# Deeper prefetch in the last loop of a hybrid encoder block: more buffers, gathered weights in halves, five splits on VectorE, a later fetch of the residual

## The chip, the cores and the metric

The kernel runs on one core of one Trainium2 chip. The metric is device time in microseconds of one execution; the median of several executions counts, and a profiled execution shows where the time goes.

## The reference

One encoder layer works on 512 tokens of width 1024, in float32. A mixer (a gated linear recurrence and a long convolution, merged by gates) adds to the tokens, then a PEER layer adds to them, then a last RMS norm follows. The change touches the PEER layer:

```python
def block(xb):
    T = xb.shape[0]
    qh = (xb @ w_q).astype(jnp.float32).reshape(T, PEER_HEADS, 2, PEER_QDIM // 2)
    s = jnp.einsum('thpc,hpnc->thpn', qh, sk)
    s1, i1 = lax.top_k(s[:, :, 0], PEER_TOPK)
    s2, i2 = lax.top_k(s[:, :, 1], PEER_TOPK)
    ...
    top_s, pos = lax.top_k(cand_s, PEER_TOPK)
    experts = jnp.take_along_axis(cand_i, pos, axis=-1)
    g = jax.nn.softmax(top_s, axis=-1).astype(xb.dtype)
    u = jnp.take(u_tab, experts, axis=0)
    v = jnp.take(v_tab, experts, axis=0)
    act = jax.nn.gelu(jnp.einsum('td,thkd->thk', xb, u)) * g
    return jnp.einsum('thk,thkd->td', act, v)
```

Each token picks 128 of 16384 experts (8 heads, 16 each). An expert is one row of table u and one row of table v, both of 1024 numbers.

## The kernel before

The 512 tokens are four blocks of 128. Three of them (`DTB`, 384 tokens) are computed densely: every expert is applied to every token, and a table of gates, zero where an expert was not chosen, weighs the result. The 16384 experts are 128 rows of 128 (`NK`); two rows are a pair, so there are 64 pairs. The fourth block (`GTB`) is computed by gathering: for each of the 128 choices of a token one row of u, later one row of v, comes by an indirect DMA.

For a row r, `act_row` loads a block of u (`uraw`), splits it into a high and a low part (`uh` on ScalarE, `ul` on VectorE, or on GpSimd once `looping` holds something), runs 24 matmuls into `ps_a` and writes the gelu of the result to `gact`. The ring for these results has eight tiles of a pair each. 22 pairs (`kept`, every third) are computed first and parked in DRAM; the others stay in the ring.

`gates_out` writes the gates of the dense blocks to DRAM as `Gd`. In the last loop `gated(p)` loads a block of gates `gt` (one for two pairs) and, for a kept pair, `gkept`; it multiplies both in place (L1013) and splits the product into `gh` and `gl`. `split_v(r)` loads row r of table v (`vraw`) and splits it into `vh` and `vl`, three rows ahead. `combine(r)` runs 18 matmuls into the six accumulators `acc`. Thus a plain row of the loop is 18 matmuls, and one with an act row 42; 70 of the act rows lie in the loop, over its first 120 rows. Six (`LEFT`) come just ahead of it: this stretch, in which the choice of the gathered block's experts (`select`) also runs on VectorE, is called the bridge below.

`gathered()` is the other side of the loop. It ends the choice for block `GTB`, then asks for the gathered rows, four ahead, one indirect DMA of GpSimd each, and works them up on VectorE: 128 dot products into `gdot` (L978), one gelu and one product with the gates (L980, L981), then 128 multiply-adds into `gacc` (L985, L987). `weave` runs both sides: each value that `rows()` yields lets through as many steps of `gathered()` as it counts, 2.08 (`WEIGHT`) for every row of the loop.

After the last act row `fetch_residual` asks for the final norm's weights and for the four blocks of tokens on ScalarE's queue. `summed` and `scaled` add, norm and store at the end.

The order on each engine is laid by a scheduler that estimates times: an instruction can stand ahead of one that the program names earlier, but each engine's queue, SP's list of DMA requests too, then runs strictly in its order, and an instruction that waits holds all behind it. A buffer of a pool is given again only when the last reader of its former tile is done. `issue_after` ties the gathers to the latest split on GpSimd.

Of the kernel before, what the change touches and what calls it, by code (L numbers as in the profile page):

```python
# [21 lines left out]
P = 128  # L22
# [795 lines left out]
GTB = 0  # L818
# [25 lines left out]
def peer(C, ctx, mh, ml):  # L844
# [4 lines left out]
    xg = cp.tile([P, D], F32, name="xg")  # L849
    gate = cp.tile([P, TB, P], F32, name="gate")  # L850
    eid = cp.tile([P, TB, P], F32, name="eid")
    v16 = cp.tile([P, TB, 16, TOPK], F32, name="v16")
    i16 = cp.tile([P, TB, 16, TOPK], U32, name="i16")
    pio = cp.tile([P, NPAIR, TOPK // 2], BF16, name="pio")
    with tc.tile_pool(name="pid", bufs=1) as ip:
        pid = ip.tile([P, NPAIR], F32, name="pid")
        nc.scalar.dma_start(pid, a["pair"].to_broadcast([P, NPAIR]))
        nc.vector.tensor_copy(pio, pid[:, :, None].to_broadcast([P, NPAIR, TOPK // 2]))
    iota = cp.tile([P, P, 4], BF16, name="iota")
    nc.gpsimd.iota(iota, pattern=[[1, P], [0, 4]], base=0, channel_multiplier=0, allow_small_or_imprecise_dtypes=True)  # L860
    gidx = cp.tile([P, P], I32, name="gidx")
    gdot = cp.tile([P, P], F32, name="gdot")
    gw = cp.tile([P, P], F32, name="gw")
    def chosen(pool, tb, part, ahead=2):
        return select(C, pool, tb, part, v16, i16, gate, eid, pio, ahead)

# [3 lines left out]
    puctx = ExitStack()  # L870
    sgctx = ExitStack()
    pu = puctx.enter_context(tc.tile_pool(name="pu", bufs=UB, side="right"))
    s0 = sgctx.enter_context(tc.tile_pool(name="sg", bufs=1, side="right")).tile([P, 16, P], F32, name="s0")
    acts, factors, looping = {}, {}, []
    anchor = [None]
    last_gelu = [None]
# [26 lines left out]
            nc.scalar.dma_start(C.kept[kept.index(r // 2)], acts.pop(r // 2))  # L903

    NP = NK // 2
    kept = [p for p in range(NP) if (p + 1) * KEPT // NP > p * KEPT // NP]
    order = [r for r in range(NK) if r // 2 in kept] + [r for r in range(NK) if r // 2 not in kept]

    def act_rows():
# [10 lines left out]
    with tc.tile_pool(name="gb", bufs=1) as gb, tc.tile_pool(name="slw", bufs=2) as sw, \  # L920
            tc.tile_pool(name="go", bufs=3) as go, tc.tile_pool(name="ps_g", bufs=5, space=PSUM) as ps_g:
        def best(pool):
            for hp in range(16):
                top16(C, pool, v16[:, GTB, hp], i16[:, GTB, hp], s0[:, hp])
                if hp % 2:
                    yield 0.4

        def weighed(tb, parts):
            for part in parts:
                for c in chosen(sw, tb, part):  # L930
                    yield CHOICE * c
# [27 lines left out]
    def gathered():  # L959

        for part in range(2):
            yield from chosen(sw, GTB, part, 1)
        nc.vector.tensor_copy(gidx, eid[:, GTB])
        swctx.close()
        gp = rowctx.enter_context(tc.tile_pool(name="gp", bufs=GBUFS))
        asked = chain(((a["u"], j) for j in range(P)), ((a["v"], j) for j in range(P)))
        there = []
        for q in islice(asked, GAHEAD):
            there.append(gather(gp, *q))
            yield 1.2  # L970

        def row():
            there.extend(gather(gp, *q) for q in islice(asked, 1))
            return there.pop(0)

        for j in range(P):
            t = row()
            nc.vector.scalar_tensor_tensor(t, t, 1.0, xg, op0=ALU.mult, op1=ALU.mult, accum_out=gdot[:, j : j + 1])  # L978
            yield 1.2
        nc.scalar.activation(gw, gdot, AF.Gelu_apprx_tanh)  # L980
        nc.vector.tensor_mul(gw, gw, gate[:, GTB])  # L981
        for j in range(P):
            t = row()
            if j == 0:
                nc.vector.tensor_scalar(gacc, t, gw[:, 0:1], None, op0=ALU.mult)  # L985
            else:
                nc.vector.scalar_tensor_tensor(gacc, t, gw[:, j : j + 1], gacc, op0=ALU.mult, op1=ALU.add)  # L987
            yield 1.2

    prep = {}  # L990
# [1 line left out]
    def split_v(r):  # L992
# [4 lines left out]
        split(nc, vh, vl, raw)  # L997
        prep[r] = vh, vl

    def gated(p):  # L1000

        r = 2 * p
        if r % GR == 0:
            gt = pg.tile([P, NG, GR * GQ], F32, name="gt")
            nc.sync.dma_start(gt, C.Gd[:, :, r * GQ : (r + GR) * GQ].rearrange("g p x -> p g x"))
            prep["gt"] = gt.rearrange("p g (r t) -> p r g t", t=GQ)
        if p in kept:
            g = pg.tile([P, 2, ND], F32, name="gkept", bufs=1)
            nc.sync.dma_start(g, C.kept[kept.index(p)])
        else:  # L1010
            g = acts.pop(p)
        g4 = g.rearrange("p r (g t) -> p r g t", t=GQ)
        nc.vector.tensor_mul(g4, g4, prep["gt"][:, r % GR : r % GR + 2])  # L1013
        gh = pg.tile([P, 2, ND], F32R, name="gh", bufs=3)
        gl = pg.tile([P, 2, ND], F32R, name="gl", bufs=3)
        split(nc, gh, gl, g)
        prep["g", p] = gh, gl
# [12 lines left out]
    def rows():  # L1030
        for r in range(AHEAD - 1):
            split_v(r)
        for _ in range(LEFT - 1):
            act_row()
            yield 2.4
        gated(0)
        act_row()
        split_v(AHEAD - 1)
        gated(1)
        yield 2.4  # L1040
        n = len(order)
        for r in range(NK):
            while order and (n - len(order)) * (NK - END) < (r + 1) * n:
                act_row()
                if not order:
                    log_table(C, last_gelu[0])
                    puctx.close()
                    fetch_residual()
            if r + AHEAD < NK:
                split_v(r + AHEAD)  # L1050
            if r % 2 == 0 and r // 2 + 2 < NP:
                gated(r // 2 + 2)
            if r < NK - LAST:
                combine(r)
            elif r == NK - 1:
                for k in range(len(DTB)):
                    for c in range(2):
                        for q in range(NK - LAST, NK):
                            combine(q, (k,), (c,))
            yield WEIGHT  # L1060

    fin = {}

    def fetch_residual():
        fin["pool"] = fp = rowctx.enter_context(tc.tile_pool(name="fin", bufs=1, side="right"))
        fin["g"] = gf = fp.tile([P, D], F32, name="gf")
        nc.scalar.dma_start(gf, a["g_fin"].to_broadcast([P, D]))
        for tb in range(TB):
            fin[tb] = fp.tile([P, D], F32, name=f"ht{tb}")
            nc.scalar.dma_start(fin[tb], C.hd[tb * P : tb * P + P])  # L1070

    looping.append(True)
    weave(rows(), gathered(), 1.0)


# [60 lines left out]
def queries(C, xh, xl, v16, i16, s0, chosen, fill):  # L1136
# [3 lines left out]
    with tc.tile_pool(name="slc", bufs=1) as cp, tc.tile_pool(name="slw0", bufs=2) as w2, tc.tile_pool(name="slw1", bufs=2) as sw:  # L1140
# [3 lines left out]
        def scores(hp, ps):  # L1144
            qT = w2.tile([P, L], F32, name="qT")
            nc.scalar.copy(qT, ps)
            pt = C.ps_s.tile([P, 512], F32, name="ps_s")
            for tb in range(TB):
                nc.tensor.matmul(pt[:, tb * P : tb * P + P], qT[:, tb * P : tb * P + P], sk[:, hp], start=True, stop=True)
            pt = pt.rearrange("p (t n) -> p t n", t=TB)  # L1150
            s = w2.tile([P, len(DTB), P], F32, name="s")
            nc.scalar.copy(s, pt[:, DTB[0] : DTB[-1] + 1])
            nc.scalar.copy(s0[:, hp], pt[:, GTB])
            for k, tb in enumerate(DTB):
                top16(C, w2, v16[:, tb, hp], i16[:, tb, hp], s[:, k])

        early = chain(*(chosen(sw, tb, 0) for tb in DTB[:EARLY]))
        for hp in range(16):
# [30 lines left out]
def select(C, w2, tb, part, v16, i16, gate, eid, pio, ahead=2):  # L1189
# [3 lines left out]
    hs = slice(part * 2 * H, part * 2 * H + 2 * H)  # L1193
    ks = slice(part * H * TOPK, part * H * TOPK + H * TOPK)
    i16f = w2.tile([P, 2 * H, TOPK], F32, name="i16f")
    nc.vector.tensor_copy(i16f, i16[:, tb, hs])
    ctop = w2.tile([P, H, TOPK], F32, name="ctop")
    cpos = w2.tile([P, H, TOPK], U32, name="cpos")
    cs = w2.tile([P, H, NPAIR], F32, name="cs")
    ci = w2.tile([P, H, NPAIR], F32, name="ci")  # L1200
    i1x = w2.tile([P, H, TOPK], F32, name="i1x")
    vv = v16[:, tb, hs].rearrange("p (h q) k -> p h q k", q=2)
    ii = i16f.rearrange("p (h q) k -> p h q k", q=2)
    nc.vector.tensor_scalar(i1x, ii[:, :, 0], 128.0, None, op0=ALU.mult)
    for dst, x1, x2, groups in ((cs, vv[:, :, 0], vv[:, :, 1], pair_groups(0, TOPK)[0]), (ci, i1x, ii[:, :, 1], FIRST + OTHERS)):
# [216 lines left out]
```

## Time and profile before

| | |
|---|---|
| median of 3 runs | 2085.55 us (2085.42 to 2086.84) |
| profiled execution | 2092.13 us |
| its span | 2090.4 us |
| first matmul into acc | 1250.5 us |
| last matmul into acc | 2083.0 us |
| granted TensorE clock, mean | 0.994 |

In the profile, PE is the matmuls of TensorE, PEld its weight loads, DVE is VectorE, ACT ScalarE, POOL GpSimd and SP the engine that only issues DMAs. Times count from the start of the span. A row of a timeline gives start and duration in us, the engine, the line, the operation, out<-in with shapes, and in brackets the idle time ahead of it with what ended it. A row of waits gives who waited for whom, the total in us, how often, and the longest. What a profiled execution takes above the median is not told apart by stage.

### The profile page before, as it was taken

Reading aid. Unit: us, or ns where it says so; the run is one execution under the profiler, and the core shown is the slowest. Engines: PE = TensorE matmul, PEld = TensorE weight load, DVE = VectorE, ACT = ScalarE, POOL = GpSimd, SP = SyncE. Lnnn points to the kernel's source line nnn. Section 1 sums busy time; section 2 is a strip of 40 time slices with the busy share of each in tenths; the row PEclk is TensorE's granted clock in tenths of the full one; section 3 lists DMA queues with packets and bytes.
Section 4 is the critical chain, followed back from the end, with each engine's and each line's share of the span. In section 5 each row is a group of like instructions: output and inputs, shape, how many; then the busy total and the mean of one; then the engine's idle time right before and its main releaser. Section 6 shows DMA issues by size and latency. Waiting matters only on the chain. (4 is left out here: it accounts for less than half of the span.)

```text
span 2090.4 us, 30873 instructions
## 1 busy us (share of the span) xinstructions
PE 2040.2 (98%) x11625; PEld 1791.7 (86%) x11625; DVE 1680.3 (80%) x3094; ACT 988.9 (47%) x1432; POOL 568.9 (27%) x336
## 2 busy tenths in 40 slices
PE   8999999999999999999999989999999999999996
PEld 6888888777777898889999988888888888888885
DVE  6788864898998647979999777897776787888795
ACT  5555434667766623436776643333333224333332
POOL 0000000000000000000000047767676666766860
PEclk9999999999999999999999999999999999999998
DMA  5212213122112444224556688999988998999984
GB/s 191 81 51 66 71 61 100 61 71 72 61 61 82 133 151 139 91 74 163 214 190 241 244 262 306 339 328 327 330 322 293 334 336 303 347 345 341 332 325 160
DMA packets 157844, 417.97 MB, mean 200 GB/s; under 512 B 12891, under 2 KB 66013, under 8 KB 156031
## 3 DMA queue, kind: packets, MB, share of 16 engines
q1 hardware_dynamic: 111900, 260.96, 36.4%
q0 software_dynamic: 36864, 134.23, 17.3%
q10 hardware_dynamic: 8930, 20.81, 2.8%
q8 instruction: 91, 1.49, 0.3%
q14 instruction: 59, 0.48, 0.1%
HBM read 377.94 MB, written 38.01 MB: 199 GB/s over the span
## 5 line engine op out<-in xcount | busy, mean ns | idle before, releaser
L93 POOL TENSOR_TENSOR ul<-uraw,uh 128x1024 fp32r<-128x1024 f32 x75 | 201.3, 2685 | 636.7 <-ACT uh L92 632.0
L101 PE MATMUL ps_a<-pxh,uh 128*128 128x384 f32 x1024 | 347.9, 340 | 8.4 <-ACT gact L901 8.4
L102 PE MATMUL ps_a<-pxl,uh 128*128 128x384 f32 x1024 | 345.1, 337 | 0.0
L1027 PE MATMUL acc<-vl,gh 128*128 128x512 f32 x768 | 302.1, 393 | 14.1 <-DVE vl L93 14.1
L1028 PE MATMUL acc<-vh,gl 128*128 128x512 f32 x768 | 302.0, 393 | 0.0
L1026 PE MATMUL acc<-vh,gh 128*128 128x512 f32 x768 | 300.4, 391 | 0.0
L92 ACT CAST vh<-vraw 128x1024 fp32r<-128x1024 f32 x128 | 134.6, 1051 | 350.3 <-DMA vraw<-in_v 241.3
L101 PE MATMUL ps_mm<-xh,whi 128*128 128x512 f32 (+1 forms) x656 | 256.9, 393 | 0.6 <-ACT gt L254 0.4
L102 PE MATMUL ps_mm<-xl,whi 128*128 128x512 f32 (+1 forms) x656 | 255.4, 391 | 0.0
L987 DVE SCALAR_TENSOR_TENSOR xg<-grow,gw,xg 128x1024 f32<-128x1024 f32 x127 | 188.9, 1487 | 57.3 <-DMA grow<-in_v,gidx 55.7
L978 DVE SCALAR_TENSOR_TENSOR grow<-grow,xg 128x1024 f32<-128x1024 f32 x128 | 177.8, 1406 | 53.6 <-DMA grow<-in_u,gidx 53.3
L101 PEld LDWEIGHTS ps_a<-pxh,uh 128*128 128x128 f32 x1024 | 193.2, 189 | 12.9 <-ACT gact L901 9.9
L860 POOL IOTA iota<- 128x512 bf16 x1 | 1.2, 1236 | 744.3 <-DVE gt L295 744.3
L955 POOL DMA_INDIRECT grow<-in_u,gidx x128 | 188.7, 1474 | 46.9 <-issue 22.3
L104 PE MATMUL ps_a<-pxh,ul 128*128 128x384 f32 x1024 | 198.2, 334 | 0.0
L102 PEld LDWEIGHTS ps_a<-pxl,uh 128*128 128x128 f32 x1024 | 193.2, 189 | 3.0
L92 ACT CAST whi<-wraw 128x1024 fp32r<-128x1024 f32 x112 | 117.5, 1050 | 156.6 <-PE ps_mm L102 133.6
L955 POOL DMA_INDIRECT grow<-in_v,gidx x128 | 177.4, 1386 | 38.6 <-issue 20.2
L93 DVE TENSOR_TENSOR vl<-vraw,vh 128x1024 fp32r<-128x1024 f32 x128 | 182.4, 1426 | 4.6 <-ACT vh L92 4.6
L1027 PEld LDWEIGHTS acc<-vl,gh 128*128 128x128 f32 x768 | 145.2, 189 | 43.9 <-DVE vl L93 14.9
L92 ACT CAST uh<-uraw 128x1024 fp32r<-128x1024 f32 x128 | 134.4, 1050 | 96.4 <-PE ps_a L102 66.8
L104 PEld LDWEIGHTS ps_a<-pxh,ul 128*128 128x128 f32 x1024 | 179.3, 188 | 0.1
(409 smaller groups left out, 4103.9 us busy)
## 6 DMA issues: line engine op xcount, KB each, us to landing
uraw<-in_uT SPq DMA_DIRECT2D x128, 512.0 KB, 5.6
vraw<-in_v SPq DMA_DIRECT2D x128, 512.0 KB, 6.4
wraw<-in_w_in SPq DMA_DIRECT2D x80, 512.0 KB, 3.6
Gd<-Gs SPq DMA_DIRECT2D x12, 2048.0 KB, 7.8
gt<-Gd SPq DMA_DIRECT2D x32, 768.0 KB, 8.9
kept<-gact ACTq DMA_DIRECT2D x22, 384.0 KB, 3.7
gkept<-kept SPq DMA_DIRECT2D x22, 384.0 KB, 5.1
wraw<-in_w_q SPq DMA_DIRECT2D x16, 512.0 KB, 4.6
```

Of the source, the lines that this page charges most:

```text
L92: nc.scalar.copy(hi, src)
L93: return (eng or nc.vector).tensor_sub(lo, src, hi).ins
L101: nc.tensor.matmul(out, ah, bh, start=(i == 0), stop=False)
L102: nc.tensor.matmul(out, *((al, bh) if late else (ah, bl)), start=False, stop=False)
L104: nc.tensor.matmul(out, *((ah, bl) if late else (al, bh)), start=False, stop=(stop and i == n - 1))
L860: nc.gpsimd.iota(iota, pattern=[[1, P], [0, 4]], base=0, channel_multiplier=0, allow_small_or_imprecise_dtypes=True)
L955: nc.gpsimd.indirect_dma_start(out=t, out_offset=None, in_=tab, in_offset=bass.IndirectOffsetOnAxis(ap=gidx[:, j : j + 1], axis=0))
L978: nc.vector.scalar_tensor_tensor(t, t, 1.0, xg, op0=ALU.mult, op1=ALU.mult, accum_out=gdot[:, j : j + 1])
L987: nc.vector.scalar_tensor_tensor(gacc, t, gw[:, j : j + 1], gacc, op0=ALU.mult, op1=ALU.add)
L1026: nc.tensor.matmul(acc[k][c], gh[:, ts_], vh[:, ds_], start=(r == 0), stop=False)
L1027: nc.tensor.matmul(acc[k][c], gh[:, ts_], vl[:, ds_], start=False, stop=False)
L1028: nc.tensor.matmul(acc[k][c], gl[:, ts_], vh[:, ds_], start=False, stop=(r == NK - 1))
```

## The change

Only the PEER layer changes.

- `gt` has three buffers in place of two and `gkept` two in place of one. Their loads move out of `gated` into `fetched(p)`, which is called four pairs ahead (`FETCH`); the first four calls stand ahead of `gated(0)`.
- The first and second best of the dense blocks (`v16`, `i16`) and `iota` move to a pool that is closed before the last loop.
- The list of kept pairs is mirrored: 0, 3, ... 61 in place of 2, 5, ... 63.
- `looping` is set after `gated(0)` in place of before the bridge, so the splits that the first five of the six bridge rows ask for run on VectorE.
- A row of the loop yields in proportion to its estimated matmul time, with the same total.
- `gdot` and `gw` are halves of 64 columns, each with its own gelu and its own product with the gates, the product 16 rows later.
- `fetch_residual` is called behind `split_v(127)`, and issues on SP.

```diff
 WEIGHT = 2.08
+COMB = 18 * 227
+ACTR = 24 * 173
...
+FETCH = 4
+LATER = 16
...
-    v16 = cp.tile([P, TB, 16, TOPK], F32, name="v16")
-    i16 = cp.tile([P, TB, 16, TOPK], U32, name="i16")
+    v16 = {GTB: cp.tile([P, 16, TOPK], F32, name="v16g")}
+    i16 = {GTB: cp.tile([P, 16, TOPK], U32, name="i16g")}
...
-    iota = cp.tile([P, P, 4], BF16, name="iota")
-    nc.gpsimd.iota(iota, pattern=[[1, P], [0, 4]], base=0, channel_multiplier=0, allow_small_or_imprecise_dtypes=True)
...
-    gdot = cp.tile([P, P], F32, name="gdot")
-    gw = cp.tile([P, P], F32, name="gw")
+    gdot = [cp.tile([P, P // 2], F32, name=f"gdot{h}") for h in range(2)]
+    gw = [cp.tile([P, P // 2], F32, name=f"gw{h}") for h in range(2)]
...
-    s0 = sgctx.enter_context(tc.tile_pool(name="sg", bufs=1, side="right")).tile([P, 16, P], F32, name="s0")
+    sg = sgctx.enter_context(tc.tile_pool(name="sg", bufs=1, side="right"))
+    for tb in DTB:
+        v16[tb] = sg.tile([P, 16, TOPK], F32, name=f"v16{tb}")
+        i16[tb] = sg.tile([P, 16, TOPK], U32, name=f"i16{tb}")
+    iota = sg.tile([P, P, 4], BF16, name="iota")
+    nc.gpsimd.iota(iota, pattern=[[1, P], [0, 4]], base=0, channel_multiplier=0, allow_small_or_imprecise_dtypes=True)
+    s0 = sg.tile([P, 16, P], F32, name="s0")
...
-    kept = [p for p in range(NP) if (p + 1) * KEPT // NP > p * KEPT // NP]
+    kept = [p for p in range(NP) if (NP - p) * KEPT // NP > (NP - 1 - p) * KEPT // NP]
...
+        half = P // 2
+
+        def weigh(h):
+            nc.vector.tensor_mul(gw[h], gw[h], gate[:, GTB, h * half : h * half + half])
+
         for j in range(P):
             t = row()
-            nc.vector.scalar_tensor_tensor(t, t, 1.0, xg, op0=ALU.mult, op1=ALU.mult, accum_out=gdot[:, j : j + 1])
+            h, i = divmod(j, half)
+            nc.vector.scalar_tensor_tensor(t, t, 1.0, xg, op0=ALU.mult, op1=ALU.mult, accum_out=gdot[h][:, i : i + 1])
+            if i == half - 1:
+                nc.scalar.activation(gw[h], gdot[h], AF.Gelu_apprx_tanh)
+            if j == half + LATER:
+                weigh(0)
             yield 1.2
-        nc.scalar.activation(gw, gdot, AF.Gelu_apprx_tanh)
-        nc.vector.tensor_mul(gw, gw, gate[:, GTB])
         for j in range(P):
...
+            if j == LATER:
+                weigh(1)
             yield 1.2
...
+    def fetched(p):
+
+        r = 2 * p
+        if p < NP and r % GR == 0:
+            gt = pg.tile([P, NG, GR * GQ], F32, name="gt", bufs=3)
+            nc.sync.dma_start(gt, C.Gd[:, :, r * GQ : (r + GR) * GQ].rearrange("g p x -> p g x"))
+            prep["gt", r // GR] = gt.rearrange("p g (r t) -> p r g t", t=GQ)
+        if p in kept:
+            g = prep["k", p] = pg.tile([P, 2, ND], F32, name="gkept")
+            nc.sync.dma_start(g, C.kept[kept.index(p)])
+
     def gated(p):
 
         r = 2 * p
-        if r % GR == 0:
-            gt = pg.tile([P, NG, GR * GQ], F32, name="gt")
-            nc.sync.dma_start(gt, C.Gd[:, :, r * GQ : (r + GR) * GQ].rearrange("g p x -> p g x"))
-            prep["gt"] = gt.rearrange("p g (r t) -> p r g t", t=GQ)
-        if p in kept:
-            g = pg.tile([P, 2, ND], F32, name="gkept", bufs=1)
-            nc.sync.dma_start(g, C.kept[kept.index(p)])
-        else:
-            g = acts.pop(p)
+        g = prep.pop(("k", p)) if p in kept else acts.pop(p)
+        gt = prep["gt", r // GR]
...
         for _ in range(LEFT - 1):
             act_row()
             yield 2.4
+        for p in range(FETCH):
+            fetched(p)
         gated(0)
+        looping.append(True)
         act_row()
         split_v(AHEAD - 1)
         gated(1)
         yield 2.4
         n = len(order)
+        share = (WEIGHT * NK) / (COMB * NK + ACTR * n)
         for r in range(NK):
+            time = COMB
             while order and (n - len(order)) * (NK - END) < (r + 1) * n:
                 act_row()
+                time += ACTR
                 if not order:
                     log_table(C, last_gelu[0])
                     puctx.close()
-                    fetch_residual()
             if r + AHEAD < NK:
                 split_v(r + AHEAD)
-            if r % 2 == 0 and r // 2 + 2 < NP:
-                gated(r // 2 + 2)
+            if r + AHEAD == NK - 1:
+                fetch_residual()
+            if r % 2 == 0:
+                fetched(r // 2 + FETCH)
+                if r // 2 + 2 < NP:
+                    gated(r // 2 + 2)
...
-            yield WEIGHT
+            yield share * time
...
-        nc.scalar.dma_start(gf, a["g_fin"].to_broadcast([P, D]))
+        nc.sync.dma_start(gf, a["g_fin"].to_broadcast([P, D]))
         for tb in range(TB):
             fin[tb] = fp.tile([P, D], F32, name=f"ht{tb}")
-            nc.scalar.dma_start(fin[tb], C.hd[tb * P : tb * P + P])
-
-    looping.append(True)
+            nc.sync.dma_start(fin[tb], C.hd[tb * P : tb * P + P])
+
     weave(rows(), gathered(), 1.0)
```

More of the change, by code (lines that the diff above doesn't have):

```diff
@@ L923, in best @@
             for hp in range(16):
-                top16(C, pool, v16[:, GTB, hp], i16[:, GTB, hp], s0[:, hp])
+                top16(C, pool, v16[GTB][:, hp], i16[GTB][:, hp], s0[:, hp])
                 if hp % 2:
@@ L974, in row @@
             return there.pop(0)
+        half = P // 2
+        def weigh(h):
+            nc.vector.tensor_mul(gw[h], gw[h], gate[:, GTB, h * half : h * half + half])
         for j in range(P):
             t = row()
-            nc.vector.scalar_tensor_tensor(t, t, 1.0, xg, op0=ALU.mult, op1=ALU.mult, accum_out=gdot[:, j : j + 1])
+            h, i = divmod(j, half)
[4 more added lines that the diff above has]
+                weigh(0)
             yield 1.2
-        nc.scalar.activation(gw, gdot, AF.Gelu_apprx_tanh)
-        nc.vector.tensor_mul(gw, gw, gate[:, GTB])
         for j in range(P):
             t = row()
+            h, i = divmod(j, half)
             if j == 0:
-                nc.vector.tensor_scalar(gacc, t, gw[:, 0:1], None, op0=ALU.mult)
+                nc.vector.tensor_scalar(gacc, t, gw[0][:, 0:1], None, op0=ALU.mult)
             else:
-                nc.vector.scalar_tensor_tensor(gacc, t, gw[:, j : j + 1], gacc, op0=ALU.mult, op1=ALU.add)
+                nc.vector.scalar_tensor_tensor(gacc, t, gw[h][:, i : i + 1], gacc, op0=ALU.mult, op1=ALU.add)
+            if j == LATER:
+                weigh(1)
             yield 1.2
@@ L998, in split_v @@
         prep[r] = vh, vl
+    def fetched(p):
[7 more added lines that the diff above has]
+            nc.sync.dma_start(g, C.kept[kept.index(p)])
     def gated(p):
         r = 2 * p
-        if r % GR == 0:
-            gt = pg.tile([P, NG, GR * GQ], F32, name="gt")
-            nc.sync.dma_start(gt, C.Gd[:, :, r * GQ : (r + GR) * GQ].rearrange("g p x -> p g x"))
-            prep["gt"] = gt.rearrange("p g (r t) -> p r g t", t=GQ)
-        if p in kept:
-            g = pg.tile([P, 2, ND], F32, name="gkept", bufs=1)
-            nc.sync.dma_start(g, C.kept[kept.index(p)])
-        else:
-            g = acts.pop(p)
+        g = prep.pop(("k", p)) if p in kept else acts.pop(p)
+        gt = prep["gt", r // GR]
         g4 = g.rearrange("p r (g t) -> p r g t", t=GQ)
-        nc.vector.tensor_mul(g4, g4, prep["gt"][:, r % GR : r % GR + 2])
+        nc.vector.tensor_mul(g4, g4, gt[:, r % GR : r % GR + 2])
         gh = pg.tile([P, 2, ND], F32R, name="gh", bufs=3)
@@ L1154, in scores @@
             for k, tb in enumerate(DTB):
-                top16(C, w2, v16[:, tb, hp], i16[:, tb, hp], s[:, k])
+                top16(C, w2, v16[tb][:, hp], i16[tb][:, hp], s[:, k])
         early = chain(*(chosen(sw, tb, 0) for tb in DTB[:EARLY]))
@@ L1195, in select @@
     i16f = w2.tile([P, 2 * H, TOPK], F32, name="i16f")
-    nc.vector.tensor_copy(i16f, i16[:, tb, hs])
+    nc.vector.tensor_copy(i16f, i16[tb][:, hs])
     ctop = w2.tile([P, H, TOPK], F32, name="ctop")
@@ L1201, in select @@
     i1x = w2.tile([P, H, TOPK], F32, name="i1x")
-    vv = v16[:, tb, hs].rearrange("p (h q) k -> p h q k", q=2)
+    vv = v16[tb][:, hs].rearrange("p (h q) k -> p h q k", q=2)
     ii = i16f.rearrange("p (h q) k -> p h q k", q=2)
```

## The prediction

> **What bounds the kernel now.** I read the page first, then busy time by stage, then the waits of TensorE, then what stands behind each wait.
>
> ```profile
> span 2090.4 us, 30873 instructions
> PE 2040.2 (98%) x11625; PEld 1791.7 (86%) x11625; DVE 1680.3 (80%) x3094; ACT 988.9 (47%) x1432; POOL 568.9 (27%) x336
> ```
>
> TensorE is busy for 98% of the span, and the change removes no matmul. It can only win what TensorE loses in the stretch that the change touches, the bridge into the last loop (from about 1200) and that loop. Busy time in steps of 5 us shows the losses (columns: busy us and count of PE, PEld, DVE, ACT, POOL; then granted clock, DMA share, GB/s):
>
> ```profile
> 1205.00:1210.00 5.00, 4.14 (x24) 3.82 (x23) 5.00 (x37) 2.38 (x3) 0.00 (x0) 1.00 0.78 261
> 1215.00:1220.00 5.00, 4.10 (x24) 3.78 (x23) 5.00 (x11) 2.88 (x5) 1.11 (x1) 1.00 0.96 349
> 1225.00:1230.00 5.00, 2.12 (x13) 1.80 (x11) 5.00 (x6) 0.00 (x0) 2.11 (x1) 1.00 0.89 258
> 1230.00:1235.00 5.00, 2.85 (x9) 2.85 (x10) 5.00 (x9) 2.55 (x4) 1.89 (x1) 0.74 0.51 174
> 1630.00:1635.00 5.00, 1.35 (x8) 0.97 (x7) 3.44 (x5) 1.53 (x2) 1.06 (x1) 1.00 0.66 236
> 1635.00:1640.00 5.00, 5.00 (x16) 3.93 (x17) 5.00 (x7) 0.25 (x1) 4.00 (x3) 0.66 1.07 339
> 1250.00:2045.00 795.00, 791.35 (x3855) 702.22 (x3854) 640.92 (x613) 271.31 (x320) 547.60 (x324) 1.00 0.91 328
> 2045.00:2050.00 5.00, 0.81 (x4) 0.34 (x2) 2.15 (x2) 0.70 (x1) 0.00 (x0) 0.82 0.89 356
> 2050.00:2055.00 5.00, 0.00 (x0) 0.00 (x0) 3.83 (x5) 1.58 (x2) 0.00 (x0) 0.50 0.04 15
> 2055.00:2060.00 5.00, 3.78 (x9) 3.00 (x10) 4.40 (x7) 1.36 (x7) 0.00 (x0) 0.50 0.50 142
> 2060.00:2065.00 5.00, 5.00 (x20) 4.02 (x19) 4.29 (x5) 2.66 (x3) 0.00 (x0) 0.82 0.80 279
> 2083.40:2090.40 7.00, 0.00 (x0) 0.00 (x0) 2.26 (x5) 1.22 (x4) 0.00 (x0) 0.67 0.40 150
> ```
>
> A loss is the idle time plus the busy time times what is missing of the clock. **Bridge**: idle 0.86 + 0.90 + 2.88 + 2.15 = 6.8, and 0.26 x 2.85 = 0.7 of clock, 7.5 us. **Middle**: idle 3.65, clock 0.34 x 5.00 = 1.7, 5.35 us; the long row (795 us, idle 3.65) says that this is the loop's only stall before 2045. **End**: idle 4.19 + 5.00 + 1.22 = 10.4, clock 0.50 x 3.78 + 0.18 x 5.00 = 2.8, 13.2 us. Together 26 us: no version of this change can win more. The last 7.0 us, after the last matmul, are not touched: the sum, square, scale and store of the last block keep their order.
>
> Each loss has a different cause. In the bridge VectorE has no idle time, and part of its work is waiting (timelines of VectorE, GpSimd and ScalarE; start, duration, instruction):
>
> ```profile
> 1213.48 2.63 POOL L93 TENSOR_TENSOR ul<-uraw,uh 128x1024 fp32r<-128x1024 f32 x1 [467.49 <-ACT uh L92]
> 1220.90 6.21 POOL L93 TENSOR_TENSOR ul<-uraw,uh 128x1024 fp32r<-128x1024 f32 x2 [4.79 <-ACT uh L92]
> 1209.31 0.94 DVE L1013 TENSOR_TENSOR gact<-gact,gt 128x768 f32<-128x768 f32 x1
> 1211.60 1.21 DVE L93 TENSOR_TENSOR ul<-uraw,uh 128x1024 fp32r<-128x1024 f32 x1
> 1213.96 2.97 DVE L1013 TENSOR_TENSOR gact<-gact,gt 128x768 f32<-128x768 f32 x1
> 1230.88 0.83 ACT L92 CAST gh<-gkept 128x768 fp32r<-128x768 f32 x1 [7.31 <-DVE gkept L1013]
> ```
>
> The gate product (L1013) takes 0.94 alone and 2.97 when it starts under a GpSimd ul. ScalarE then waits 7.31 us for such a product, and behind that wait stands the gelu that frees a ps_a buffer for TensorE. Middle and end are transfers that come late:
>
> ```profile
> 1616.92 14.55 DMA gkept<-kept
> 1631.56 0.96 DVE L1013 TENSOR_TENSOR gkept<-gkept,gt 128x768 f32<-128x768 f32 x1 [7.46 <-DMA gkept<-kept]
> SPq L1005 <- DVE gkept L1013: 63.7, 14, 13.6
> 2033.21 17.63 DMA grow<-in_v,gidx
> 2051.12 1.04 ACT L92 CAST vh<-vraw 128x1024 fp32r<-128x1024 f32 x1 [5.42 <-DMA vraw<-in_v]
> 2053.74 1.29 DVE L1085 TENSOR_TENSOR ht<-ht,xg 128x512 f32<-128x512 f32 x2 [0.20 <-DVE xg L987]
> 2054.95 2.35 DVE L93 TENSOR_TENSOR vl<-vraw,vh 128x1024 fp32r<-128x1024 f32 x2
> ```
>
> In the middle the single gkept buffer is reloaded only when its last reader is done; the load takes 14.55 us, VectorE stands still for 7.46 of them, and SP, which waits for that product to free a gt buffer (13.6 at the longest), holds the next v rows. At the end the last gathered row takes 17.63 us, and the vl that TensorE needs stand behind the last gather and the sum of block 0 on VectorE.
>
> **The change part by part.**
>
> *End.* I weigh transfers of 2029 to 2051 (the DMA view of that window):
>
> ```profile
> DMA packets 2252, 8.05 MB, mean 366 GB/s; under 512 B 259, under 2 KB 259, under 8 KB 2251
> q10 hardware_dynamic: 720, 2.62, 32.0%
> ```
>
> Of 8.05 MB, 2.62 (q10, ScalarE's queue) are fetch_residual: g_fin and four ht. Moved behind the request for the last v row, they leave this place: 2.62 MB / 366 GB/s = 7.2 us. The new yields count too. Before, a row of the loop lets 2.08 steps of the gather through whether or not it holds an act row. Now the share is 2.08 x 128 / (4086 x 128 + 4152 x 70) = 3.27e-4 per ns: 1.34 steps for a plain row, 2.70 for a row with an act. The last 8 rows have no act: 10.7 steps in place of 16.6, so about 5.9 gathers of 134.22 / 256 = 0.52 MB come earlier:
>
> ```profile
> q0 software_dynamic: 36864, 134.23, 17.3%
> ```
>
> That is 3.1 MB, 8.5 us at 366 GB/s. Both together relieve 15.7 us where 10.4 were idle, with 5 to spare. The last kept pair is 61 in place of 63, so no gkept load is due in the last rows. What is late next: the residual itself on SP. It goes out when vl of row 124 is done, seven rows of 4.09 us before the end, 28 us for 7.2 us of transfers. I take 11.5 of 13.2 us won; the bounds are 13.2 (all) and 4 (the rows' own loads stay late).
>
> The Trainium skill (DMA: Bandwidth & Descriptors, section Issuing engines are not separate DMA queues) speaks against one half: a queue is no bandwidth of its own, requests of all engines run on the same 16 DMA engines. The move from ScalarE to SP alone would then be worth nothing; this sum takes its 7.2 us from the later time, not from the queue.
>
> *Middle.* gkept gets a second buffer, gt a third, and both are asked four pairs ahead of use rather than two. The load no longer waits for its predecessor's reader, so 14.55 us of transfer have some three pairs (3 x 2 rows x about 6.3 us, 795 us over some 126 rows) to hide in. I take 4.5 of 5.35: a new, shorter stall elsewhere is likely where DMA is 0.91 busy. Bounds: 5.35 won, and 5.5 lost if one such stall more appears.
>
> *Bridge.* looping is set after gated(0), so five ul (those of the LEFT - 1 act rows) go from GpSimd to VectorE: 5 x 1.21 = 6.1 us more there. What VectorE then no longer waits for: the product above, 2.97 - 0.94 = 2.0 us, and these:
>
> ```profile
> 1222.79 2.08 DVE L1235 TENSOR_TENSOR one<-pio,cpf 128x320 bf16<-128x320 bf16 x1
> 1219.51 0.80 DVE L1235 TENSOR_TENSOR one<-pio,cpf 128x320 bf16<-128x320 bf16 x2
> 1225.68 1.93 DVE L1237 TENSOR_TENSOR exp<-one,ci 128x320 f32<-128x320 bf16 x1
> 1195.78 0.71 DVE L1237 TENSOR_TENSOR exp<-one,ci 128x320 f32<-128x320 bf16 x1
> 1233.00 4.00 DVE L1013 TENSOR_TENSOR gact<-gact,gt 128x768 f32<-128x768 f32 x2
> ```
>
> 2.08 - 0.40, 1.93 - 0.71 and 4.00 - 2 x 0.94 make 1.7 + 1.2 + 2.1; with the first 7.0 us. VectorE gains about 1 us net, and TensorE gets ul in 1.21 rather than 2.63 us. The larger part is order: ScalarE's instruction for gh was queued as if VectorE had been done 7 us earlier, and without the waits under GpSimd that slip shrinks. Against it: four pairs' fetches stand ahead of gated(0), so gkept of pair 0 and of pair 3 and the second gt, up to 1.6 MB or 4 us at the rate above, go among the u and v rows. I take 5 of 7.5 won, nearest to the row of 7.31; bounds 7.5 won and 3 lost (4 us of late u rows less 1 us).
>
> Stalls that only shrink save more than their idle time: the row of 1205 (0.86 idle, clock 1.00) lost no clock, the one at the end did. The Trainium skill (TensorE: Matmul & The Clock Gate, section What's actually happening) says that the clock halves after an idle window of about 3.4 us. The trace agrees (0.86 keeps 1.00, over 10 us give 0.50); by that rule a bridge stall (2.88 + 2.15 in a row) cut under 3.4 would win its 0.7 of clock too, which the 5 us hold already.
>
> *Nothing.* Halves of the gathered weights: the switch to table v has ScalarE wait 5.40 us, but the long row holds no TensorE idle time there; one small gelu and one small product more lie beside VectorE's idle time (640.92 busy of 795). v16 and i16 by block, the moved iota (GpSimd is otherwise empty until 1213) and the mirrored kept pairs run the same instructions; 32 gt and 22 gkept loads stay. If the cover on VectorE is gone, the halves cost under 1 us.
>
> **Sum.** 11.5 + 4.5 + 5 = 21 us from the profiled execution's 2092.13 (span 2090.4, 1.7 around it): 2071. The median of the plain runs, 2085.55, is 6.6 lower; some of that may be stall that those runs never had, so I take 19.5 from it: **2066**.
>
> **Rivals.**
> 1. *The bridge is not relieved* (VectorE stays full, early fetches delay the u rows): the bridge's 5 us are missing (2071) or turn into 3 lost (2074), and where the middle's bound comes with it, 5 to 6 us more: to 2080. For it: VectorE at 5.00 of 5 in every bridge row; against it: the 2.97 and 2.08 rows.
> 2. *The stall moves*: 0.91 of DMA is busy at 328 GB/s whatever is prefetched, so another transfer is late where the old one was; within 4 us of 2085.5. For it: one stall of 14.55 from a load of 384 KB; against: the relieved 15.7 us at the end leave the loop's last stretch.
> 3. *The queue alone was changed*, by the skill's rule in the part on the end: the residual still lands in the crowd, and the gathers' 8.5 us alone do not cover 10.4; the end keeps 2 to 5 us, 2069 to 2071. It lies inside the forecast's range.
> 4. *Slower: SP is blocked more often.* Fetches stand earlier in SP's order; each that waits for a buffer holds the v rows behind it. Price 5.35 us for a block of 13.6, the middle's row. With 19.5 to win it decides from five such blocks in the loop's 54 fetches; eight give 8 x 5.35 - 19.5 = 23 lost, 2109; six give 2098. Against it: a third gt and a second gkept buffer are free sooner.
>
> **How the numbers follow.** Forecast (with rival 3 inside): 2058 to 2074, 0.62. Rival 1: 0.18. Rival 2: 0.12, of it 0.01 on either side of the bound. Rival 4: 0.08. A measurement of this kernel can tell 0.2%, 4.2 us, from no change: faster 0.81, same 0.10, slower 0.09. The range leaves out rival 4 and about half of rival 2, and takes 26 us as its far end: 2058 to 2083.
>
> **What would show it.** End: TensorE busy through to the last matmul, the longest wait for vl under 3 us, no residual among the gathers. Middle: VectorE's waits for gkept near none. Bridge: no GpSimd ul before the sixth act row, L1013 at 0.94, ScalarE's wait for gh under 3 us. Wrong would be: waits of SP for gt buffers above 13.6 us, a wait of TensorE for ps_a before 1250 longer than 5 us, or vl behind the sum of block 0 again.

## The result, and the profile after

| | before | after |
|---|---|---|
| median of 6 runs | 2087.19 us (2085.42 to 2092.48) | 2073.43 us (2069.57 to 2076.36) |
| ratio | | 0.9932, 95% interval 0.9919 to 0.9946 |
| profiled execution, span | 2092.13, 2090.4 us | 2076.36, 2074.6 us |
| last matmul into acc | 2083.0 us | 2067.2 us |

The change wins 13.8 us. (Three more executions of before joined the three that stand above; its median rose by 1.6 us.) Busy time by stage of the changed kernel answers the rows shown of before (columns: busy us and count of PE, PEld, DVE, ACT, POOL, granted clock, DMA share, GB/s):

```profile
1195.00:1245.00 50.00, 48.22 (x273) 47.10 (x272) 41.14 (x71) 24.07 (x31) 8.23 (x5) 1.00 0.96 312
1200.00:1205.00 5.00, 3.31 (x20) 2.99 (x19) 5.00 (x7) 4.50 (x5) 0.00 (x0) 1.00 1.06 341
1410.00:1415.00 5.00, 3.36 (x15) 2.44 (x13) 2.23 (x3) 1.32 (x3) 4.82 (x3) 1.00 0.79 296
1435.00:1440.00 5.00, 3.81 (x19) 3.09 (x18) 5.00 (x7) 1.06 (x1) 2.21 (x2) 1.00 1.02 400
1250.00:2045.00 795.00, 786.84 (x3824) 694.79 (x3823) 663.04 (x621) 265.30 (x325) 534.39 (x319) 1.00 0.91 327
2025.00:2067.40 42.40, 42.40 (x191) 35.23 (x189) 27.22 (x33) 16.46 (x31) 0.00 (x0) 1.00 0.46 173
```

In the bridge TensorE is idle for 1.78 us, almost all in one place at 1202. The last 42.4 us are full: TensorE is busy for 42.40 of them at full clock. But the middle is idle for 8.16 us (795 - 786.84), where it was 3.65. Two rows of TensorE's waits over the whole span of the changed kernel (who waited for whom, total us, times, longest; of the second row one wait of 1.7 lies in the bridge, the other ahead of it), and VectorE's waits for the loads of the gate products:

```profile
PE acc L1050 <- DVE vl L93: 8.1, 7, 2.2
PE ps_a L101 <- ACT gact L909: 3.3, 2, 1.7
```

```profile
DVE gkept L1036 <- DMA gkept<-kept: 39.6, 11, 7.5
```

The one stall of 3.7 has become seven of at most 2.2, and none of them cost clock: the rows of 1410 and 1435, where two of them lie, keep 1.00.

For the experiments I count the loss from the starts of the matmuls: from 1195 on, each interval from one start to the next less 0.227 us (into acc) or 0.173 us (into ps_a), the usual spacing of the two kinds. The bridge ends with the first matmul into acc, the end is the last 45 us. About 4 us in the middle are no stall: the kernel without any wait there counts 4.14. The count includes slow clock. All rows come from one profiled execution each; the ratio is to the runs of before on the same chip. Medians between chips differ by some us, so ratios are compared.

| kernel | bridge | middle | end | ratio (95%) | median us |
|---|---|---|---|---|---|
| before | 9.5 | 9.7 | 13.3 | 1 | 2087.2 |
| after | 2.4 | 15.4 | 0.0 | 0.9932 (0.9919 to 0.9946) | 2073.4 |
| after2 (the same kernel) | 6.0 | 10.9 | 0.0 | 0.9938 (0.9920 to 0.9955) | 2073.3 |
| u_bridge | 2.4 | 6.0 | 0.0 | 0.9924 (0.9904 to 0.9945) | 2072.7 |
| u_pace | 2.4 | 7.3 | 0.0 | 0.9933 (0.9909 to 0.9957) | 2073.2 |
| u_resid | 5.6 | 6.3 | 0.0 | 0.9921 (0.9899 to 0.9942) | 2071.7 |
| u_fetch | 2.3 | 21.4 | 1.7 | 0.9965 (0.9950 to 0.9979) | 2080.6 |
| b_only | 2.3 | 6.1 | 8.0 | 0.9955 (0.9939 to 0.9971) | 2078.3 |
| f_only | 3.4 | 4.1 | 11.1 | 0.9945 (0.9924 to 0.9965) | 2077.8 |
| u_end | 3.5 | 8.1 | 7.3 | 0.9978 (0.9961 to 0.9996) | 2083.2 |
| m_only | 9.3 | 10.3 | 6.4 | 1.0013 (0.9996 to 1.0030) | 2089.7 |
| f_resid | 2.8 | 9.3 | 1.3 | 0.9919 (0.9901 to 0.9937) | 2069.9 |
| f_resid_b | 4.9 | 4.1 | 1.6 | 0.9929 (0.9908 to 0.9950) | 2069.3 |
| k_one | 1.7 | 16.3 | 0.0 | 0.9935 (0.9916 to 0.9955) | 2076.3 |

### The profile page after: what moved, and what is told of

Its sections match the earlier page's. It is cut to its first block, busy times and chain, and to the rows that moved or that the text cites. A ratio compares the mean times of both kernels' runs of the same rounds, so it can differ in the third digit from the quotient of the medians.

```text
span 2074.6 us, 30832 instructions
## 1 busy us (share of the span) xinstructions
PE 2036.9 (98%) x11625; PEld 1786.7 (86%) x11625; DVE 1699.4 (82%) x3100; ACT 983.5 (47%) x1433; POOL 548.5 (26%) x331
## 4 chain that ended last, share of the span: by engine, by line
PE 75%; DVE 11%; DMA 6%; issue 5%; ACT 2%; POOL 1%; DVEq 0%; SPq 0%; ACTq 0%; POOLq 0%
PE ps_mm L101 10%; PE ps_mm L102 10%; PE ps_mm L104 10%; PE acc L1050 6%; PE acc L1051 6%; PE acc L1049 6%; PE ps_a L102 6%; PE ps_a L101 6%; PE ps_a L104 5%; PE ps_g L1322 2%; DMA grow<-in_u,gidx 2%; PE ps_x L665 2%; DVE grow L992 2%; DMA vraw<-in_v 1%; PE ps_x L101 1%
## 5 line engine op out<-in xcount | busy, mean ns | idle before, releaser
L93 POOL TENSOR_TENSOR ul<-uraw,uh 128x1024 fp32r<-128x1024 f32 x70 | 183.7, 2625 | 591.9 <-DMA gt<-Gd 442.6
L1004 DVE SCALAR_TENSOR_TENSOR xg<-grow,gw,xg 128x1024 f32<-128x1024 f32 x127 | 204.4, 1610 | 36.7 <-DMA grow<-in_v,gidx 35.1
L992 DVE SCALAR_TENSOR_TENSOR grow<-grow,xg 128x1024 f32<-128x1024 f32 x128 | 191.7, 1518 | 44.3 <-DMA grow<-in_u,gidx 44.2
L93 DVE TENSOR_TENSOR vl<-vraw,vh 128x1024 fp32r<-128x1024 f32 x128 | 166.7, 1303 | 6.5 <-ACT vh L92 6.5
L93 DVE TENSOR_TENSOR wlo<-wraw,whi 128x1024 fp32r<-128x1024 f32 x112 | 136.4, 1218 | 43.1 <-ACT whi L92 27.8
## 6 DMA issues: line engine op xcount, KB each, us to landing
gt<-Gd SPq DMA_DIRECT2D x32, 768.0 KB, 10.3
```

The source lines that it names most:

```text
L93: return (eng or nc.vector).tensor_sub(lo, src, hi).ins
L1004: nc.vector.scalar_tensor_tensor(gacc, t, gw[h][:, i : i + 1], gacc, op0=ALU.mult, op1=ALU.add)
```

## The experiments

### One part of the change undone

**u_bridge**: the five splits on GpSimd again.

```diff
         gated(0)
-        looping.append(True)
         act_row()
...
+    looping.append(True)
     weave(rows(), gathered(), 1.0)
```

> The changed kernel with looping set ahead of the bridge again, so the five bridge splits are on GpSimd. Theory (GpSimd makes VectorE wait, ScalarE's gh and with it the gelu wait for VectorE): the bridge's loss between 1195 and 1245 goes from 2.4 back to 8 or more, products of L1036 take over 2 us there again, and the median is 5 to 8 us above the changed kernel's 2073.4. Rival (the bridge gained from the earlier fetches and the mirrored kept pairs): the loss there stays under 4 and the median within 2 us.

The theory missed: bridge 2.4, ratio as the whole change. GpSimd does slow VectorE there, and nothing comes of it (timelines of u_bridge, GpSimd then VectorE):

```profile
1221.10 7.33 POOL L93 TENSOR_TENSOR ul<-uraw,uh 128x1024 fp32r<-128x1024 f32 x3 [2.47 <-ACT uh L92]
1221.38 2.42 DVE L1279 TENSOR_TENSOR gate<-ex,sm 128x64 f32<-128x64 f32 x1
1223.73 2.44 DVE L971 CAST gidx<-eid 128x128 int32<-128x128 f32 x1
1226.08 3.43 DVE L93 TENSOR_TENSOR vl<-vraw,vh 128x1024 fp32r<-128x1024 f32 x1
```

The reason is seen earlier on VectorE: the choice of block 0's experts starts ten microseconds sooner. Its first instruction in before, in the changed kernel, in b_only (below) and in u_fetch:

```profile
1182.92 0.23 DVE L1196 CAST i16f<-i 128x128 f32<-128x128 uint32 x1 [1.40 <-PE ps_g L1291]
```
```profile
1173.45 0.22 DVE L1227 CAST i16f<-i16g 128x128 f32<-128x128 uint32 x1
```
```profile
1184.45 0.23 DVE L1196 CAST i16f<-i 128x128 f32<-128x128 uint32 x1 [1.40 <-PE ps_g L1291]
```
```profile
1181.97 0.23 DVE L1227 CAST i16f<-i16g 128x128 f32<-128x128 uint32 x1 [1.40 <-PE ps_g L1322]
```

Without the larger prefetch buffers it waits for a matmul of gates_out; with them it does not. The pool of those buffers is opened ahead of the choice's scratch, so a larger one moves the scratch to another place in memory. That the place is the cause is argued, not shown, since addresses are not in the profile. That the start goes with the buffers is shown by all fourteen profiles: 1172.8 to 1174.4 in the nine with two gkept buffers, 1180.7 to 1184.9 in the five with one (before, b_only, m_only, u_fetch and k_one). One buffer decides it: k_one, below, differs from the changed kernel by the second gkept buffer alone, and starts late:

```profile
1184.88 0.23 DVE L1227 CAST i16f<-i16g 128x128 f32<-128x128 uint32 x1 [1.40 <-PE ps_g L1322]
```

**u_pace**: 2.08 steps a row again.

```diff
-            yield share * time
+            yield WEIGHT
```

> The changed kernel with 2.08 steps of the gather for every row of the loop again. Theory (pace and residual both relieve the end): a wait for vl of 2 to 6 us comes back in the last 40 us, the middle stays as it is, median 3 to 7 us above 2073.4. Rival A (the new pace makes the seven small stalls of 1350 to 1600): the middle's loss falls from 11 to under 6 and the median is 0 to 5 us lower. Rival B (the residual alone was the end): no stall at the end, median within 2 us.

The theory missed: nothing comes back at the end. Rival B fits the end (0.0) and the time (0.9933). Rival A's middle came down to 7.3 in the profiled execution, but the median did not follow.

**u_resid**: the residual behind the last act row, on ScalarE's queue.

```diff
                     puctx.close()
+                    fetch_residual()
...
-            if r + AHEAD == NK - 1:
-                fetch_residual()
...
-        nc.sync.dma_start(gf, a["g_fin"].to_broadcast([P, D]))
+        nc.scalar.dma_start(gf, a["g_fin"].to_broadcast([P, D]))
...
-            nc.sync.dma_start(fin[tb], C.hd[tb * P : tb * P + P])
+            nc.scalar.dma_start(fin[tb], C.hd[tb * P : tb * P + P])
```

> The changed kernel with the residual asked for right behind the last act row and on ScalarE's queue again. Theory: 2.62 MB or 7.2 us of transfers come back among the last gathers, but the pace keeps 5 us spare, so a wait of 0 to 4 us for vl at the end, median 0 to 5 us above 2073.4. Rival (the residual was the whole cause): the end loses 8 us or more again, median 8 to 13 above.

No wait at the end, nothing lost in the median: of the two reliefs of the end, the pace alone is enough.

**u_fetch**: two gt buffers, one gkept buffer, loads asked for beside gated(p).

```diff
-            gt = pg.tile([P, NG, GR * GQ], F32, name="gt", bufs=3)
+            gt = pg.tile([P, NG, GR * GQ], F32, name="gt")
...
-            g = prep["k", p] = pg.tile([P, 2, ND], F32, name="gkept")
+            g = prep["k", p] = pg.tile([P, 2, ND], F32, name="gkept", bufs=1)
...
-        for p in range(FETCH):
-            fetched(p)
+        fetched(0)
         gated(0)
...
+        fetched(1)
         gated(1)
...
-                fetched(r // 2 + FETCH)
                 if r // 2 + 2 < NP:
+                    fetched(r // 2 + 2)
                     gated(r // 2 + 2)
```

> The changed kernel with two gt buffers, one gkept buffer and the loads asked for beside gated(p), two pairs ahead, as before. Theory of the prediction (the deeper prefetch removes the stall of the middle): a stall of 3 us or more for a late gkept comes back between 1250 and 2045, median 3 to 6 us above 2073.4. Rival (the product is laid on VectorE as soon as its load is expected, so more buffers only move the wait; it waits 39.6 us for gkept with them and 37.7 without): the waits stay at 35 to 45 us, the middle's loss is anywhere from 5 to 15, median within 3 us or lower.

Of the parts undone alone, this is the only one whose loss the runs show: 0.9965 against 0.9932, or 7 us where the prediction's theory gave 3 to 6. The direction fits that theory, the mechanism does not. VectorE's waits for the loads in u_fetch, and the longest of them on its timeline:

```profile
DVE gact L1036 <- DMA gt<-Gd: 31.7, 7, 8.8
DVE gkept L1036 <- DMA gkept<-kept: 26.0, 9, 5.3
```
```profile
1677.05 0.96 DVE L1036 TENSOR_TENSOR gact<-gact,gt 128x768 f32<-128x768 f32 x1 [8.82 <-DMA gt<-Gd]
```

The waits for gkept are shorter than in the changed kernel (26.0 against 39.6), against both expectations. Those for gt are new: 31.7, where the changed kernel has none. TensorE feels them: behind the one of 8.8 us and the work that it holds up on VectorE comes a wait of TensorE for vl of 3.9, behind one of 4.7 (at 1430) a wait of 2.8.

### One part alone, and both reliefs of the end undone

**b_only**: before, with looping set after gated(0).

```diff
         gated(0)
+        looping.append(True)
         act_row()
...
-    looping.append(True)
     weave(rows(), gathered(), 1.0)
```

> The kernel before, with looping set after gated(0) and nothing else changed: five splits of the bridge on VectorE. Theory now (the bridge is relieved twice over, by these splits and by the larger prefetch buffers, which move the scratch of block 0's choice to memory that is free sooner): this alone brings the bridge's loss from 9.5 to under 4, end (13.3) and middle unchanged, median 5 to 8 us below the kernel before. Rival (the splits do nothing, as undoing them cost nothing): the loss stays at 8 or more, median within 2 us of before.

The theory holds for the bridge: it goes from 9.5 to 2.3, and the ratio shows 0.45% won. The profiled end was 8.0 and not 13.3, and the median lies 8.9 us below before on the same chip, a little more than expected. Here the choice still starts late (1184.45), so the splits do it by themselves.

**f_only**: before, with the pool move, fetched, three gt and two gkept buffers; the edits are those of the change's diff for these names, and no others.

```diff
+            gt = pg.tile([P, NG, GR * GQ], F32, name="gt", bufs=3)
...
+            g = prep["k", p] = pg.tile([P, 2, ND], F32, name="gkept")
...
+        for p in range(FETCH):
+            fetched(p)
         gated(0)
...
+                fetched(r // 2 + FETCH)
```

> The kernel before, with the pool move, fetched four pairs ahead, three gt and two gkept buffers, and nothing else: splits of the bridge on GpSimd, old pace, residual, halves and kept list as before. Theory: block 0's choice starts on VectorE near 1173 instead of 1183, the bridge's loss is under 4 though GpSimd slows products there; the end still loses 8 or more unless the prefetch cures it; median 6 to 12 us below before. Rival (the place in memory does not matter): the bridge loses 8 or more, median within 4 us of before.

The theory holds too: the choice starts at 1174.29, the bridge loses 3.4 with the splits on GpSimd, and no wait is left in the middle. All that TensorE waits for from 1195 on, in f_only:

```profile
PE acc L1039 <- DVE vl L93: 8.0, 1, 8.0
PE ps_a L101 <- ACT gact L909: 3.0, 1, 3.0
```

The 8.0 are the end, which the prefetch does not cure.

**u_end**: the changed kernel with the edits of u_pace and u_resid together.

```diff
-            yield share * time
+            yield WEIGHT
...
                     puctx.close()
+                    fetch_residual()
```

> The changed kernel with both reliefs of the end undone: 2.08 steps a row, the residual behind the last act row on ScalarE's queue. Theory (each of the two alone was enough, together they are the cure): the end loses 8 to 13 us again, median 8 to 12 us above the changed kernel's 2073.4. Rival (the prefetch or the mirrored kept pairs cured the end, as undoing either relief left it at 0.01): the end loses under 2, median within 2 us of 2073.4.

The theory holds: the end loses again, 7.3 us, just under the 8 that were expected, and the ratio rises to 0.9978; the median lies 9.8 us above 2073.4, inside the range. How the DMA engines stand there, u_end first, then u_pace, then u_resid (busy time by 10 us from 2025, columns as above):

```profile
2025.00:2035.00 10.00, 10.00 (x46) 8.28 (x45) 7.43 (x7) 2.84 (x3) 1.60 (x1) 1.00 1.02 408
2035.00:2045.00 10.00, 5.48 (x20) 4.14 (x19) 7.44 (x8) 2.38 (x5) 0.00 (x0) 0.81 0.47 169
```
```profile
2025.00:2035.00 10.00, 10.00 (x46) 8.29 (x45) 9.45 (x9) 0.86 (x3) 0.00 (x0) 1.00 1.03 410
2035.00:2045.00 10.00, 10.00 (x46) 8.29 (x45) 8.02 (x9) 6.59 (x11) 0.00 (x0) 1.00 0.66 231
```
```profile
2015.00:2025.00 10.00, 10.00 (x52) 8.94 (x51) 9.86 (x10) 3.57 (x4) 0.06 (x1) 1.00 0.72 267
2025.00:2035.00 10.00, 10.00 (x46) 8.29 (x45) 5.79 (x8) 4.26 (x5) 0.00 (x0) 1.00 1.00 385
```

With the late residual (u_pace) the DMA engines are as full as in u_end, yet TensorE runs on: how full they are does not tell the two apart, the order of the requests does. In u_end the residual's requests (its first is gf) go out ahead of the last gather, VectorE waits for that row, and vl stands behind it; in u_pace the last gather goes out first (u_end's rows, then u_pace's):

```profile
2021.55 0.34 ACTq L1098 DMA_DIRECT2D gf<-in_g_fin  x1
2024.74 1.86 POOL L963 DMA_INDIRECT grow<-in_v,gidx  x1 [0.59 <-issue]
2038.65 1.28 DVE L1004 SCALAR_TENSOR_TENSOR xg<-grow,gw,xg 128x1024 f32<-128x1024 f32 x1 [1.87 <-DMA grow<-in_v,gidx]
```
```profile
2021.86 1.86 POOL L963 DMA_INDIRECT grow<-in_v,gidx  x1 [0.59 <-issue]
2025.36 0.38 SPq L1099 DMA_DIRECT2D gf<-in_g_fin  x1
```

With the early gathers (u_resid) the last one goes out at 2013.36 and the residual at 2021.31, after a gap. The same order divides all fourteen profiles: the residual is asked ahead of the last gather in the five that lose 6.4 us or more at the end, and behind it in the nine that lose 1.7 or less.

**m_only**: before, with the mirrored list.

```diff
-    kept = [p for p in range(NP) if (p + 1) * KEPT // NP > p * KEPT // NP]
+    kept = [p for p in range(NP) if (NP - p) * KEPT // NP > (NP - 1 - p) * KEPT // NP]
```

> The kernel before, with the kept pairs mirrored (0, 3, ... 61) and nothing else. Theory (the list matters only as the end's last gkept load): the end loses 13 us less the 2.4 us that the load of pair 63 took, bridge and middle within their scatter, median 0 to 4 us below before. Rival (gkept of pair 2 stood behind the bridge's 7.31 us wait, and gkept of 63 behind the end): bridge under 4 and end under 5, median 10 us or more below before.

No gain: 1.0013, and the bridge's stall stays (9.3). Both theories hoped for too much. The profiled end is 6.4, but the median shows nothing of it. (By its formula the mirrored list is 0, 2, 5, 8, ... 61, not 0, 3, ... 61; the loads due in the first four pairs are those of pairs 0 and 2.)

### What is enough, and what is left in the middle

**f_resid**: f_only with the late residual.

```diff
                     puctx.close()
-                    fetch_residual()
...
+            if r + AHEAD == NK - 1:
+                fetch_residual()
...
-        nc.scalar.dma_start(gf, a["g_fin"].to_broadcast([P, D]))
+        nc.sync.dma_start(gf, a["g_fin"].to_broadcast([P, D]))
...
-            nc.scalar.dma_start(fin[tb], C.hd[tb * P : tb * P + P])
+            nc.sync.dma_start(fin[tb], C.hd[tb * P : tb * P + P])
```

> The kernel before with the pool move, the deeper prefetch and the late residual on SP, and nothing else (pace 2.08, bridge splits on GpSimd, old kept list, no halves). Theory (bridge cured by the prefetch's place in memory, end by the residual's time alone, gt waits by the third buffer): bridge 2 to 4, end under 1, middle 4 to 8 (4 is the count's floor), median 2066 to 2071, below the changed kernel's 2073.4. Rival (the end needs the new pace, or the middle's small stalls come with any kernel whose end is relieved): end 3 or more or middle 11 or more, median 2072 or above.

The prefetch with its pool move and the late residual give all of the change's gain: 0.9919, median 2069.9 within the expected range. The middle (9.3) and the end (1.3) were a little above what the theory gave.

**f_resid_b**: f_resid with the edit of b_only.

```diff
         gated(0)
+        looping.append(True)
         act_row()
```

> As f_resid, with the five bridge splits on VectorE too, so the changed kernel without new pace, halves and mirrored list. Theory (the splits have nothing left to win once the prefetch has moved block 0's choice): within 2 us of f_resid. Rival: 2 to 4 us below it.

Median 2069.3 beside 2069.9: the splits add nothing that the runs show once the prefetch is there. Neither kernel is shown to be faster than the changed one on the same chip (2073.3, after2); the intervals overlap.

**after2**: the changed kernel, no edit.

> The changed kernel itself, for a second profile. If the eleven us of small stalls between 1350 and 1600 belong to the kernel, the middle shows 13 to 17 again at the same places; if they belong to the execution (its six times spread over 7 us and the profiled one was the slowest), the middle shows 6 to 12 at other places.

The middle shows 10.9 with two waits in place of 15.4 with seven (waits of TensorE from 1195 on, after2):

```profile
PE acc L1050 <- DVE vl L93: 3.9, 2, 2.2
PE ps_a L101 <- ACT gact L909: 3.0, 1, 3.0
```

So 4.5 us of the first profile's middle belong to that execution. The bridge scatters too (6.0 against 2.4): its stall at 1202 is 3.0 us in place of 1.7, and here the clock fell behind it.

**k_one**: the changed kernel with one gkept buffer.

```diff
-            g = prep["k", p] = pg.tile([P, 2, ND], F32, name="gkept")
+            g = prep["k", p] = pg.tile([P, 2, ND], F32, name="gkept", bufs=1)
```

> The changed kernel with one gkept buffer; gt keeps three, and all is asked four pairs ahead. Theory now (the third gt buffer is what the prefetch wins, as without the prefetch VectorE waits 31.7 us for gt and with it not at all, while its waits for gkept are 39.6 with two buffers and 37.7 with one): median within 2.5 us of the changed kernel's 2073.4, no wait for gt over 3 us. The prediction's step (the second gkept buffer removes the stall): median 2078 or above, near the 2080.6 without any prefetch, with a stall of 3 us behind a gkept load.

By the median alone (2076.3) it lies between the two, 0.4 us outside the theory's range, but before ran slower on this chip too (2089.5); the ratio, 0.9935, is the changed kernel's. No stall of 3 us came back, and there is no wait for gt. VectorE's waits for loads in k_one:

```profile
DVE gkept L1036 <- DMA gkept<-kept: 35.9, 12, 5.5
```

Beside the other parts of the change, the second gkept buffer wins nothing that can be measured. That is again one of a redundant pair: without this buffer the choice starts at 1184.88, as in before, but the splits on VectorE still keep the bridge at 1.7. What it would be worth with the splits on GpSimd was not run. For the loads, the third gt buffer and the earlier asking remain of the prefetch; neither was run by itself.

## Why the prediction came out as it did

Forecast 2066, measured 2073.4, inside 2058 to 2083. Places and causes were right for the end and in part for the bridge, wrong for the middle, and the gain came out 5.7 us under the forecast (13.8 in place of 19.5). By its steps:

- *26 us is the most that can be won, and matmuls and tail do not change.* Nothing speaks against it: 13.8 were won, and the stretch after the last matmul kept its length (the spans end 7.4 us after its start in both).
- *End, 11.5 won.* Mis-sized, by a little: it won all 13.2. The reason was half right. I needed both reliefs, 15.7 us against 10.4 idle, and held one alone (7.2 or 8.5) for too little. u_pace and u_resid show 0.0 with one each, u_end shows 7.3 with neither: they are redundant. What a byte count missed is order. u_pace moves bytes at 410 GB/s where u_end does at 408, but its last gather goes out ahead of the residual.
- *Rival 3 (without the later time the end keeps 2 to 5 us)* falls with it: u_resid is that case, and keeps nothing. The Trainium skill's rule (DMA: Bandwidth & Descriptors, section Issuing engines are not separate DMA queues) that requests of all engines run on the same 16 DMA engines is not tested by a run here: u_pace and f_resid move the residual in time and to SP at once. The order of the requests goes with the cure in all profiles; what the queue alone would do stays open.
- *Bridge, 5 won.* Right in size within the scatter: by the prediction's own measure 5.7 were won in the first profile (idle time from 6.8 to 1.8, and the 0.7 of clock), 3.5 in the count of the second, so 5 lies between. The reading was right that GpSimd's splits reach TensorE through VectorE and ScalarE: b_only alone brings 9.5 to 2.3; the path itself is read from the profile of before. But I costed the pool move and the buffers at nothing here, and they cure the bridge as well (f_only: 3.4; u_bridge: 2.4); the buffer that decides when the choice starts is the second gkept (k_one). The early fetches, for which I kept 3 us of loss, cost nothing that a run separates.
- *Middle, 4.5 won.* This step failed, and it is the one that made the sum too good: by the prediction's measure the middle's loss went from 5.35 to 8.16 us in the first profile, 2.8 lost where 4.5 were to be won. It said that with a second buffer the load "has some three pairs to hide in". It has not: the gate product moves forward on VectorE with its load, so VectorE meets the load wherever it stands. From the request of a gkept on SP to its product, the median of the 22 loads is 5.5 us in before and 5.9 in after, while the product's lead over the first matmul of its pair grows from 50 to 85 us. The load of pair 20, whose first matmul starts at 1510.9 in before and at 1508.3 in after (request and product, before, then after):

```profile
1454.16 0.33 SPq L1009 DMA_DIRECT2D gkept<-kept  x1
1458.74 0.96 DVE L1013 TENSOR_TENSOR gkept<-gkept,gt 128x768 f32<-128x768 f32 x1
```
```profile
1418.69 0.33 SPq L1028 DMA_DIRECT2D gkept<-kept  x1
1424.84 0.96 DVE L1036 TENSOR_TENSOR gkept<-gkept,gt 128x768 f32<-128x768 f32 x1 [5.04 <-DMA gkept<-kept]
```

So the sign "waits for gkept near none" did not come. VectorE's waits for gkept between 1250 and 2030 add up to 27.3 to 46.0 us in the nine profiles with two buffers (39.6 in after, 40.8 in after2) and to 26.0 to 39.9 in the five with one (35.3 in before, 35.9 in k_one). What the prefetch does win is the gt waits: 31.7 us in u_fetch, which loses 0.33% of the time. It was worth its place, for another reason than the one given, and against a baseline that the other parts had made worse: before itself waited for gt only 8.3 us, and 18.9 with the mirrored list (m_only).
- *"A new, shorter stall elsewhere is likely"* came true seven times rather than once: TensorE's idle time in the middle rose from 3.65 to 8.16 us in the first profile. Rival 2 (the stall moves) held for this place alone.
- *That a shortened bridge stall also wins its clock* did not hold in every profile: after2's wait of 3.0 us was followed by a granted clock of 0.50, f_only's of 3.0 by 1.00. The last section has the rows.
- *Rival 1 and rival 4* did not come about. SP's longest wait for a gt buffer is 13.2, against 13.6 in before (the row holds the nine waits that a gkept product ended):

```profile
SPq L1024 <- DVE gkept L1036: 57.4, 9, 13.2
```

- *Halves, mirrored list: nothing.* Right for the list (m_only, 1.0013). The halves were not run alone; f_resid, without them, is not slower.

What stays open is why the changed kernel's middle waits more than f_only's (8.1 and 3.9 us against none). Undoing the pace, the splits or the residual each gave a middle of 6.0 to 7.3 in one profile, and none moved the median clearly. The two profiles of the changed kernel differ by 4.5 themselves, so the profiles do not settle it.

## What to carry to other kernels

Before summing gains, ask whether two edits cure the same stall: undoing one of a redundant pair shows nothing, so run each alone and undo both. Where an engine's order is laid by expected times, another buffer for a load helps only if the reader is not moved forward with it; look at the reader's wait and at its distance from the request, not at the load's start. A larger buffer can also move other tiles to memory that comes free at another time, so compare the start of the next work, not only the part that was edited.

## What was not expected of the hardware

- A GpSimd split slows more of VectorE than the gate products: in u_bridge the cast of gidx took 2.44 us under it, where the changed kernel's took 0.20. Both are single rows:

```profile
1220.38 0.20 DVE L971 CAST gidx<-eid 128x128 int32<-128x128 f32 x1
```

- DMA engines that are full for 10 us (1.02 and 1.03 busy, 408 and 410 GB/s) are no sign of a stall in themselves: u_pace loses nothing in the next 10, u_end 4.5.
- In the changed kernel, waits of TensorE of 2.2 us and less left the granted clock at 1.00; the 3.65 of before was followed by 0.66. At 3.0 it went either way: the stall near 1202 is 3.0 us in after2 and in f_only, and the clock behind it is 0.50 in one and 1.00 in the other, so the length of the wait alone does not decide it here. After2, then f_only (columns as above):

```profile
1207.50:1210.00 2.50, 2.50 (x10) 2.50 (x9) 2.50 (x3) 1.56 (x2) 0.00 (x0) 0.50 0.93 335
```
```profile
1207.50:1210.00 2.50, 2.50 (x16) 2.50 (x16) 2.50 (x4) 2.50 (x5) 0.00 (x0) 1.00 0.99 335
```
